# Attention on one Trainium2 core: a bank of values copied whole, its halves joined through a transfer and GpSimd, and the softmax's inverse as a power on GpSimd

## The chip, the core and the metric

The kernel runs on one core of one Trainium2 chip. Its engines are named as in the profile: PE (TensorE, matrix products and transposes through an identity matrix; PEld is its weight load), DVE (VectorE), ACT (ScalarE), POOL (GpSimd) and SP (SyncE, which here only issues transfers). Each engine works through its own list in order; an instruction that waits holds up everything behind it on its engine. SBUF and PSUM are the on-chip memories, both with 128 partitions; PE writes to PSUM. The metric is the device time of one launch in microseconds (us), as the median of several runs.

## What is computed

A two-layer encoder on 1024 tokens of width 1024. Only the attention of the first layer is touched by the change:

```python
q = rmsnorm(q, q_gain); k = rmsnorm(k, k_gain)
q = apply_axial_rope(q, cos, sin) * (HEAD_DIM ** -0.5)
k = apply_axial_rope(k, cos, sin)
...
def attend_block(q_blk):
    scores = jnp.einsum('bkgqd,bksd->bkgqs', q_blk, kt).astype(jnp.float32)
    p = jax.nn.softmax(scores, axis=-1).astype(vt.dtype)
    return jnp.einsum('bkgqs,bksd->bkgqd', p, vt)
...
return o @ w_o
```

There are 16 query heads of width 64 and four key and value heads. After it come a cross-attention and a gated feed-forward part, then a second layer with a pooling mixer; they make up most of the time, and their code is the same before and after.

## The kernel before

All products are done with numbers split in two: `hi` is the value rounded to PE's reduced float32 form, `lo` is the rest, and a product is made of the partial products that matter.

The attention loop works on 128 **units**. A unit is one query head for one block of 128 queries; the units 2n and 2n+1 are the same head for two blocks. Helper `skewed` runs three stages with a lag: in step s it writes down `scores(s)`, then `turn_p(s-2)`, then `values(s-3)`, and the last does something for odd units only, for both blocks of a head at once.

- `scores(u)`: PE makes four products into a PSUM tile `pA` (128 queries by 1024 keys, two such tiles; line 779). DVE takes the row maximum (789), ACT takes the exponential into an SBUF tile `scr` and sums each row at the same time (792), DVE takes the inverse of the sum (794), POOL multiplies the rows by it (795).
- `turn_p(u)`: PE turns the 128 by 1024 probabilities in eight transposes into two banks `pB` (740); ACT writes the `hi` part (673) and DVE the `lo` part (674) of each bank into `PT`.
- `values(u)`, u odd: PE multiplies `PT` with the values of the head in 16 products into one bank `pB` of 128 partitions by 256 queries (1191, 1192). The weights hold the `hi` part of the values in 64 columns and the `lo` part in the other 64, so the head's result is the sum of the upper and lower 64 partitions. ACT copies the lower half to SBUF (1196) and DVE adds the upper half from PSUM to it (1197). The two heads of a pair share one tile `osum`, an even head in partitions 0 to 63 and an odd one in 64 to 127. After an odd head POOL writes the pair's `hi` (1200) and `lo` (1201).

Inside the loop the order on each engine is that of the program as the tile framework lays it out, with its own look ahead; there are no due times here. Transfers are all issued from SP. At the loop's end SP issues the eight loads of the output projection's weights `w_o` (681, each 512 KB through a `scr` tile, then split by ACT and DVE) and the eight loads of the residual `X` (2122). Pool `scr` has six tiles of 128 by 1024. The output projection runs in the order: rows 0 and rows 2 with the first four weight loads, then rows 0 and rows 2 with the last four.

Of the kernel before, what the change touches and what calls it, by code (L numbers as in the profile page):

```python
# [10 lines left out]
F32 = mybir.dt.float32  # L11
F32R = mybir.dt.float32r
AF = mybir.ActivationFunctionType
OP = mybir.AluOpType
AX = mybir.AxisListType

P = 128
# [6 lines left out]
HD = 64  # L24
# [55 lines left out]
def skewed(n, *stages):  # L80

    for step in range(n + max(lag for lag, _ in stages)):
        for lag, stage in stages:
            if 0 <= step - lag < n:
                stage(step - lag)


class Slots:


    def __init__(self, tiles):
        self.tiles = tiles
        self.freed = {(i, h): 0 for i in range(len(tiles)) for h in range(2)}
        self.clock, self.now, self.until = 0, None, None
# [534 lines left out]
class Kernel:  # L629
    def __init__(self, ctx, tc, a, out):  # L630
        self.ctx, self.tc, self.nc, self.a, self.out = ctx, tc, tc.nc, a, out
        pool = lambda name, **k: ctx.enter_context(tc.tile_pool(name=name, bufs=1, **k))
        self.cst = pool("cst")
        self.rp = pool("rslots")
        self.fp = pool("fp")
        self.st = pool("st")
        self.R = Slots([self.rp.tile([P, 2048], F32R, name=f"R{i}") for i in range(N_SLOTS)])
        nc = self.nc
        self.ident = self.cst.tile([P, P], F32, name="ident")
        make_identity(nc, self.ident)  # L640
        self.WT = {}
        self.mh = self.cst.tile([P, 8], F32, name="mh")
        nc.vector.memset(self.mh, -0.5)
        nc.scalar.activation(self.cst.tile([P, 8], F32, name="warm"), self.mh, AF.Square)


# [115 lines left out]
    def attention(self):  # L762
        nc, R, a, tc = self.nc, self.R, self.a, self.tc
# [5 lines left out]
        Q, prs, OT, sums = {}, {}, [], {}  # L769

        def score(u):
            j, hh, i = units[u]
            kv = hh // 4
            c0 = (j % 2 + 2 * i) * P
            q = R.v(Q[kv, j // 2], 4)[:, hh % 4, c0:c0 + P]
            s = self.psA()
            for kh in range(2):
                for part in range(2):
                    nc.tensor.matmul(s[:, kh * 512:(kh + 1) * 512], q,  # L779
                                     R.v(K[part][kh], 4)[:, kv],  # L780
                                     start=part == 0, stop=part == 1)
            return s

        def scores(u):
            if u in prs:
                return
            s = score(u)
            nm = self.stat(1, "nm")
            nc.vector.tensor_reduce(nm, s, axis=AX.X, op=OP.max, negate=True)  # L789
            pr = prs[u] = self.scr()  # L790
            rs = self.stat(1, "sum")
            nc.scalar.activation(pr, s, AF.Exp, bias=nm, accum_out=rs)  # L792
            ri = self.stat(1, "inv")
            nc.vector.reciprocal(ri, rs)  # L794
            nc.gpsimd.tensor_scalar(pr, pr, ri, 1.0, op0=OP.mult, op1=OP.mult)  # L795

        with tc.tile_pool(name="qk", bufs=1, reuse_waits="tile") as qk, self.psum("psq", 1, 6) as self.ps:
# [3 lines left out]
            tabs, at, where = {"Q": tab}, {}, {}  # L801
# [59 lines left out]
            def plan_x(n0, wide, sizes, late=()):  # L861
                c0 = n0 % 512
                for j, w in enumerate(sizes):
                    k0 = sum(sizes[:j])
                    raw, k = ("xraw", n0, k0), ("hT", n0, k0)
                    for t in range(n0 // P, (n0 + wide) // P):
                        at["xkeys"].setdefault(t, []).extend([k] * w)

                    def fetch(raw=raw, k0=k0, w=w):
                        at[raw] = self.scr()[:, :w * wide].rearrange("p (k n) -> p k n", k=w)  # L870
                        nc.sync.dma_start(out=at[raw], in_=xt[k0 * P:(k0 + w) * P, n0:n0 + wide].rearrange("(k p) n -> p k n", p=P))

                    def parts(b):
                        return (R.v(s, 4)[:, b % 4, c0:c0 + wide] for s in hT[n0 // 512][b // 4 * 2:b // 4 * 2 + 2])

                    def high(raw=raw, k0=k0, w=w):
                        for b in range(k0, k0 + w):
                            nc.scalar.activation(list(parts(b))[0], at[raw][:, b - k0], AF.Copy, scale=at["gain"][:, b:b + 1])

                    def low(raw=raw, k0=k0, w=w):  # L880
                        for b in range(k0, k0 + w):
                            hi, lo = parts(b)
                            nc.vector.scalar_tensor_tensor(lo, at[raw][:, b - k0], at["gain"][:, b:b + 1], hi.bitcast(F32),
                                                           op0=OP.mult, op1=OP.subtract)
                        at.pop(raw)
                    plan.add("load", w * wide / 1024, fetch, (), [raw], [("scr", raw)], late=late[j] if late else None)
                    plan.add("copy", w * (wide + 100), high, [raw, "gain"], [k], uses=[raw])
                    plan.add("add", w * (wide + 60), low, [raw, k, "gain"], [k], uses=[raw])
# [280 lines left out]
        self.ps = self.ctx.enter_context(self.psum("ps", 2, 4))  # L1169
        with tc.tile_pool(name="at", bufs=1, reuse_waits="tile") as at:  # L1170
            PT = [[at.tile([P, 2048], F32R, name=f"PT{i}{j}") for j in range(2)] for i in range(2)]
            def parts(u):
                return (x.rearrange("p (a b) -> p a b", a=8) for x in PT[u // 2 % 2])

            def turn_p(u):
                ph, pl = parts(u)
                c = slice(u % 2 * P, (u % 2 + 1) * P)
                self.transposed(prs.pop(u), lambda g, p: self.hi_lo(ph[:, 4 * g:4 * g + 4, c], pl[:, 4 * g:4 * g + 4, c], p))

            def values(u):  # L1180
                j, hh, i = units[u]
                if i == 0:
                    return
                kv = hh // 4
                if hh == 0:
                    OT.append([R.get(), R.get()])
                ph, pl = parts(u)
                o = self.psB()[:, :256]
                for kt in range(NT):
                    v = R.tiles[V[kt // 4]].rearrange("p (k h c) -> p k h c", k=4, h=4)[:, kt % 4, kv, :]  # L1190
                    nc.tensor.matmul(o, v, ph[:, kt], start=kt == 0, stop=False)  # L1191
                    nc.tensor.matmul(o, v, pl[:, kt], start=False, stop=kt == NT - 1)  # L1192
                if hh % 2 == 0:
                    sums[0] = at.tile([P, 256], F32, name="osum", bufs=2)
                oo = sums[0][(hh % 2) * HD:(hh % 2 + 1) * HD]
                nc.scalar.copy(oo, o[HD:])
                nc.vector.tensor_tensor(out=oo, in0=o[:HD], in1=oo, op=OP.add)
                if hh % 2:
                    hi, lo = (R.v(x, 8)[:, hh // 2] for x in OT[j])
                    nc.gpsimd.tensor_scalar(hi, sums[0], 1.0, 1.0, op0=OP.mult, op1=OP.mult)  # L1200
                    nc.gpsimd.tensor_tensor(out=lo, in0=sums[0], in1=hi.bitcast(F32), op=OP.subtract)
                if hh % 4 == 3:
                    if j % 2:
                        R.put(Q[kv, j // 2])

            skewed(len(units), (0, scores), (2, turn_p), (3, values))
            R.put(*V, *K[0], *K[1])
        return OT
# [9 lines left out]
    def cross(self, i, X, steps=None, mixer=None, over={}):  # L1218
# [6 lines left out]
        plan_sums = self.down_sums(i)  # L1225
        q, nf, mem, kT, v, sm, PT, O, wo = {}, D // (2 * P), {}, [], [], {}, {}, {}, {}
        both = lambda t: [(f"X{t}", j) for j in range(2)]
# [158 lines left out]
        def plan_turn(plan, t):  # L1386
# [7 lines left out]
            def part(g, j):  # L1394
                if t % 2 not in PT:
                    PT[t % 2] = [R.get_pair() for _ in range(4)]
                pairs = PT[t % 2][2 * g:2 * g + 2]
                src = sm["ps", t][g].rearrange("p (a b) -> p a b", a=4)
                same = all(one[0] == other[0] for one, other in pairs[:j + 1])
                for ks in [slice(0, 4)] if same else [slice(0, 2), slice(2, 4)]:  # L1400
                    hi, lo = (R.blocks(z, ks, slice(t // 2 * P, (t // 2 + 1) * P)) for z in pairs)
                    self.low(hi, lo, src[:, ks]) if j else self.high(hi, src[:, ks])
            plan.add("turn", 8, emit, both(t), banks, [("B", k) for k in banks])
            for g in range(2):
                k = ("PT", t, g)
                plan.add("copy", 512, partial(part, g, 0), [banks[g]], [k], (), banks[g:g + 1], room=(("PT", t % 2), 8))
# [762 lines left out]
```

## Time and profile before

| what | value |
|---|---|
| median of 3 runs | 2509.84 us (2508.43 to 2512.4) |
| the profiled execution, its own time | 2511.04 us |
| its span in the trace | 2509.3 us |
| PE busy | 2480.5 us, 99% |
| DVE busy | 1982.1 us, 79% |
| ACT busy | 1354.9 us, 54% |
| POOL busy | 387.9 us, 15% |
| the attention loop's row maxima (line 789) | from 177.0 to 525.0 us |

The profile is of one execution. Shares are averages over very different stages: POOL, idle for most of the program, does half of its work in the attention loop. Ends of PE's instructions are modelled, so starts are the better guide to its pace.

### The profile page before, as it was taken

What the parts mean: (1) busy time and instruction counts of PE and PEld (TensorE: products, weight loads), DVE (VectorE), ACT (ScalarE), POOL (GpSimd) and SP (SyncE); (2) the same over time, 40 slices, a digit from 0 to 9 for tenths busy, and PEclk for the clock granted to TensorE, in tenths of its full rate; (3) what the DMA queues carried; (4) which work ended last, traced back from release to release, by engine and by line L of the source; (5) the groups of instructions that cost most, each with busy time, mean ns of one, the idle gap of its engine ahead of it and who ended that gap; (6) DMA issues with size and microseconds to landing.
All of it is one profiled execution on the core that took longest, in us unless ns stands there. A gap on an engine that the chain in (4) does not pass through costs nothing.

```text
span 2509.3 us, 37034 instructions
## 1 busy us (share of the span) xinstructions
PE 2480.5 (99%) x13435; PEld 2126.9 (85%) x13435; DVE 1982.1 (79%) x2963; ACT 1354.9 (54%) x2307; POOL 387.9 (15%) x530
## 2 busy tenths in 40 slices
PE   9999999999999999999999999999999999999998
PEld 8998888888898888888888888889888888887887
DVE  7779999974986379888889776887559988888875
ACT  6558888862555255555555334555435555555542
POOL 5755455431001000000000003102000000000001
PEclk9999999999999999999999999999999999999999
DMA  7100000042595124243358553388223324337852
GB/s 253 43 1 2 1 2 1 1 160 72 181 317 188 54 82 126 84 121 111 85 170 290 196 178 111 124 283 307 73 72 109 114 84 124 108 93 257 275 189 97
DMA packets 309613, 322.29 MB, mean 128 GB/s; under 512 B 13110, under 2 KB 243742, under 8 KB 309430
## 3 DMA queue, kind: packets, MB, share of 16 engines
q1 hardware_dynamic: 309429, 319.92, 39.4%
q8 instruction: 106, 1.74, 0.3%
q14 instruction: 78, 0.63, 0.1%
HBM read 232.48 MB, written 82.58 MB: 126 GB/s over the span
## 4 chain that ended last, share of the span: by engine, by line
PE 85%; DVE 6%; issue 4%; ACT 3%; DMA 2%; POOL 1%; POOLq 0%; SPq 0%; DVEq 0%; ACTq 0%
PE pB L746 21%; PE pB L748 21%; PE pB L747 21%; PE pA L779 4%; PE pB L740 3%; PE pA L748 3%; PE pA L746 3%; PE pA L747 3%; PE pB L1191 2%; PE pB L1192 2%; DVE R L668 1%; DVE nm L789 1%; ACT R L665 1%; PE pB L323 1%; DMA X<-in_ffn_w_up 1%
## 5 line engine op out<-in xcount | busy, mean ns | idle before, releaser
L746 PE MATMUL pB<-R,R 128*128 128x512 f32 (+1 forms) x2764 | 1025.3, 371 | 7.3 <-DVE scr L439 2.3
L748 PE MATMUL pB<-R,R 128*128 128x512 f32 (+1 forms) x2760 | 1017.6, 369 | 1.3 <-DVE R L668 1.2
L747 PE MATMUL pB<-R,R 128*128 128x512 f32 (+1 forms) x2764 | 1018.5, 368 | 0.0
L746 PEld LDWEIGHTS pB<-R,R 128*128 128x128 f32 x2764 | 521.8, 189 | 99.8 <-DVE scr L439 4.0
L748 PEld LDWEIGHTS pB<-R,R 128*128 128x128 f32 x2760 | 521.0, 189 | 88.9 <-DVE R L668 2.6
L747 PEld LDWEIGHTS pB<-R,R 128*128 128x128 f32 x2764 | 522.0, 189 | 85.3 <-DVE R L674 0.3
L665 ACT ACTIVATE R<-scr 128x512 fp32r<-128x512 f32 (+2 forms) x340 | 256.6, 781 | 217.2 <-DMA scr<-Gs 58.8
L668 DVE TENSOR_TENSOR R<-scr,R 128x512 fp32r<-128x512 f32 (+2 forms) x340 | 292.0, 888 | 21.0 <-ACT R L665 20.4
L668 DVE TENSOR_TENSOR R<-X,R 128x512 fp32r<-128x512 f32 x374 | 253.1, 689 | 67.4 <-ACT R L665 66.7
L665 ACT ACTIVATE R<-X 128x512 fp32r<-128x512 f32 x374 | 232.0, 630 | 134.9 <-PE pB L747 65.6
L719 POOL TENSOR_SCALAR ms<-ss 128x1 f32<-128x1 f32 (+1 forms) x53 | 12.9, 244 | 1657.8 <-ACT R L727 1281.3
L437 ACT COPY scr<-pB 128x512 f32<-128x512 f32 x156 | 91.0, 584 | 189.2 <-PE pB L748 183.2
L1760 DVE TENSOR_TENSOR X<-pB,X 128x512 f32<-128x512 f32 (+1 forms) x145 | 99.4, 687 | 85.6 <-PE pB L748 84.8
L795 POOL TENSOR_SCALAR scr<-scr,inv 128x1024 f32<-128x1024 f32 x125 | 140.7, 1126 | 164.0 <-DVE inv L794 158.9
L674 DVE TENSOR_TENSOR PT<-pB,PT 128x512 fp32r<-128x512 f32 x256 | 163.9, 681 | 1.6 <-ACT PT L673 0.6
L792 ACT ACTIVATE scr<-pA,nm 128x1024 f32<-128x1024 f32 x125 | 139.6, 1117 | 41.9 <-DVE nm L789 39.4
L789 DVE TENSOR_REDUCE nm<-pA 128x1 f32<-128x1024 f32 x125 | 152.5, 1220 | 0.4 <-PE pB L740 0.3
L746 PE MATMUL pA<-R,R 128*128 128x512 f32 (+1 forms) x420 | 150.6, 359 | 0.0
L748 PE MATMUL pA<-R,R 128*128 128x512 f32 (+1 forms) x420 | 150.3, 358 | 0.0
L747 PE MATMUL pA<-R,R 128*128 128x512 f32 (+1 forms) x420 | 150.0, 357 | 0.0
L779 PE MATMUL pA<-R,R 128*128 128x512 f32 x512 | 145.1, 405 | 0.0
L673 ACT ACTIVATE PT<-pB 128x512 fp32r<-128x512 f32 x256 | 138.8, 595 | 11.0 <-PE pB L740 8.2
(172 smaller groups left out, 3458.4 us busy)
## 6 DMA issues: line engine op xcount, KB each, us to landing
X<-in_ffn_w_up SPq DMA_DIRECT2D x82, 512.0 KB
Gs<-X SPq DMA_DIRECT2D x105, 256.0 KB
scr<-in_ffn_w_down SPq DMA_DIRECT2D x45, 512.0 KB
scr<-Gs SPq DMA_DIRECT2D x35, 512.0 KB
scr<-in_xattn_w_kv SPq DMA_DIRECT2D x32, 512.0 KB
scr<-Gs SPq DMA_DIRECT2D x42, 384.0 KB
Wt<-scr SPq DMA_DIRECT2D x44, 256.0 KB
Gs<-scr SPq DMA_DIRECT2D x42, 256.0 KB
```

The costliest lines, as they stand in the source:

```text
L665: self.nc.scalar.activation(hi, src, AF.Copy)
L668: self.nc.vector.tensor_tensor(out=lo, in0=src, in1=hi.bitcast(F32), op=OP.subtract)
L673: nc.scalar.activation(hi, src, AF.Copy)
L674: nc.vector.tensor_tensor(out=lo, in0=src, in1=hi.bitcast(F32), op=OP.subtract)
L746: mm(out, ah, bh, start=start, stop=False)
L747: mm(out, ah, bl, start=False, stop=False)
L748: mm(out, al, bh, start=False, stop=stop)
L779: nc.tensor.matmul(s[:, kh * 512:(kh + 1) * 512], q, R.v(K[part][kh], 4)[:, kv], start=part == 0, stop=part == 1)
L789: nc.vector.tensor_reduce(nm, s, axis=AX.X, op=OP.max, negate=True)
L792: nc.scalar.activation(pr, s, AF.Exp, bias=nm, accum_out=rs)
L795: nc.gpsimd.tensor_scalar(pr, pr, ri, 1.0, op0=OP.mult, op1=OP.mult)
L1760: nc.vector.tensor_tensor(out=x, in0=banks[b][:, c], in1=x, op=OP.add)
```

## The change

Three things are edited, all in the attention loop. The inverse of a row sum is now a power with exponent -1 on POOL, with a constant tile `m1`. ACT now copies the whole bank of values, 128 partitions, into a part of one `scr` tile (`halves`) that is held through the loop. A transfer on SP moves the half that lies in the wrong partitions into a tile `crossed`, and POOL adds the two halves; the sum of a pair of heads comes to lie in `total`, from which POOL makes `hi` and `lo` as before.

```diff
+        self.m1 = self.cst.tile([P, 1], F32, name="m1")
+        nc.vector.memset(self.m1, -1.0)
...
-            nc.vector.reciprocal(ri, rs)
+            nc.gpsimd.tensor_tensor(out=ri, in0=rs, in1=self.m1, op=OP.pow)
...
+            halves = self.scr().rearrange("p (a b c) -> p a b c", a=2, b=2)
...
-                if hh % 2 == 0:
-                    sums[0] = at.tile([P, 256], F32, name="osum", bufs=2)
-                oo = sums[0][(hh % 2) * HD:(hh % 2 + 1) * HD]
-                nc.scalar.copy(oo, o[HD:])
-                nc.vector.tensor_tensor(out=oo, in0=o[:HD], in1=oo, op=OP.add)
-                if hh % 2:
+                odd, pair = hh % 2, u // 4 % 2
+                if not odd:
+                    sums["crossed"] = at.tile([P, 256], F32, name="crossed", bufs=2)
+                own, far = halves[:, pair, odd], sums["crossed"]
+                nc.scalar.copy(own, o)
+                mine, other = (slice(HD * odd, HD * odd + HD), slice(HD - HD * odd, P - HD * odd))
+                nc.sync.dma_start(out=far[mine], in_=own[other])
+                total = halves[:, pair, 0]
+                nc.gpsimd.tensor_tensor(out=total[mine], in0=own[mine], in1=far[mine], op=OP.add)
+                if odd:
                     hi, lo = (R.v(x, 8)[:, hh // 2] for x in OT[j])
-                    nc.gpsimd.tensor_scalar(hi, sums[0], 1.0, 1.0, op0=OP.mult, op1=OP.mult)
-                    nc.gpsimd.tensor_tensor(out=lo, in0=sums[0], in1=hi.bitcast(F32), op=OP.subtract)
+                    nc.gpsimd.tensor_scalar(hi, total, 1.0, 1.0, op0=OP.mult, op1=OP.mult)
+                    nc.gpsimd.tensor_tensor(out=lo, in0=total, in1=hi.bitcast(F32), op=OP.subtract)
```

Lines of the changed kernel stand two to seven further down than before. Three places show what moves.

**DVE in the middle of the loop.** `nm` is the row maximum, `inv` the inverse, `osum` the halves' sum, `PT` the `lo` part; the rows cover four units. Before:

```order
L789 TENSOR_REDUCE nm<-pA 128x1
L1197 TENSOR_TENSOR osum<-pB,osum 64x256
L674 TENSOR_TENSOR PT_2587<-pB,PT_2586 128x4x128 x2
L794 RECIPROCAL inv<-sum 128x1
L789 TENSOR_REDUCE nm<-pA 128x1
L674 TENSOR_TENSOR PT_2589<-pB,PT_2588 128x4x128 x2
L794 RECIPROCAL inv<-sum 128x1
L789 TENSOR_REDUCE nm<-pA 128x1
L1197 TENSOR_TENSOR osum<-pB,osum 64x256
L674 TENSOR_TENSOR PT_2589<-pB,PT_2588 128x4x128 x2
L794 RECIPROCAL inv<-sum 128x1
```

and now:

```order
L791 TENSOR_REDUCE nm<-pA 128x1
L676 TENSOR_TENSOR PT_2589<-pB,PT_2588 128x4x128 x2
L791 TENSOR_REDUCE nm<-pA 128x1
L676 TENSOR_TENSOR PT_2589<-pB,PT_2588 128x4x128 x2
L791 TENSOR_REDUCE nm<-pA 128x1
L676 TENSOR_TENSOR PT_2591<-pB,PT_2590 128x4x128 x2
```

The inverses and the additions have left DVE; the row maxima and the `lo` parts keep their order.

**POOL in the middle of the loop**, four units with the end of a pair of heads. Before:

```order
L795 TENSOR_SCALAR scr<-scr,inv 128x1024 x4
L1200 TENSOR_SCALAR R_81<-osum 128x256
L1201 TENSOR_TENSOR R_82<-osum,R_81 128x256
L795 TENSOR_SCALAR scr<-scr,inv 128x1024 x4
L1200 TENSOR_SCALAR R_81<-osum 128x256
```

and now (796 is the power, 797 the multiplication, 1204 the addition of the halves):

```order
L796 TENSOR_TENSOR inv<-sum,m_94 128x1
L797 TENSOR_SCALAR scr<-scr,inv 128x1024
L1204 TENSOR_TENSOR scr<-scr,crossed 64x256
L796 TENSOR_TENSOR inv<-sum,m_94 128x1
L797 TENSOR_SCALAR scr<-scr,inv 128x1024
L796 TENSOR_TENSOR inv<-sum,m_94 128x1
L797 TENSOR_SCALAR scr<-scr,inv 128x1024
L1204 TENSOR_TENSOR scr<-scr,crossed 64x256
L1207 TENSOR_SCALAR R_81<-scr 128x256
L1208 TENSOR_TENSOR R_82<-scr,R_81 128x256
L796 TENSOR_TENSOR inv<-sum,m_94 128x1
L797 TENSOR_SCALAR scr<-scr,inv 128x1024
```

The addition of the halves of an odd unit u stands behind the multiplication of unit u+3 and ahead of the power of unit u+4.

**SP at the loop's end**, with buffer numbers. Before, the weights' loads stand together (the first three and the last are shown), with the residual's behind them:

```order
L681 DMA scr_7320<-in_attn_w_o 128x2x512
L681 DMA scr_7324<-in_attn_w_o 128x2x512
L681 DMA scr_7328<-in_attn_w_o 128x2x512
...
L681 DMA scr_7365<-in_attn_w_o 128x2x512
L2122 DMA X0_7339<-in_x 128x1024
```

and now, from the last crossing but one on:

```order
L1202 DMA crossed_7346<-scr_2592 64x256
L683 DMA scr_7395<-in_attn_w_o 128x2x512
L683 DMA scr_7399<-in_attn_w_o 128x2x512
L1202 DMA crossed_7346<-scr_2592 64x256
L683 DMA scr_7420<-in_attn_w_o 128x2x512
L683 DMA scr_7424<-in_attn_w_o 128x2x512
L2129 DMA X0_7406<-in_x 128x1024
...
L2129 DMA X5_7411<-in_x 128x1024
L683 DMA scr_7428<-in_attn_w_o 128x2x512
L683 DMA scr_7432<-in_attn_w_o 128x2x512
L2129 DMA X6_7412<-in_x 128x1024
```

The loads of the weights now stand behind crossings, and the last two behind six loads of the residual.

## The prediction

> **What bounds the kernel now.** I first asked for the busy time in a window inside the loop (columns: window, length, then PE, PEld, DVE, ACT and POOL busy with counts, PE's clock, DMA share, GB/s), and for the row maxima, of which each unit has one (count, then least/median/most ns, first and last start).
>
> ```profile
> 250.00:300.00 50.00, 50.00 (x359) 44.45 (x358) 47.71 (x82) 42.53 (x81) 24.52 (x26) 1.00 0.01 1
> L789 DVE TENSOR_REDUCE nm<-pA x125: 1204/1225/1227, 177.0 to 525.0; 128x1 f32<-128x1024 f32 x125
> ```
>
> PE and DVE are both near full. 124 steps in 348.0 us make 2.806 us for a unit, 11.23 us for four units, the pattern's period (two heads, one even, one odd), 31 times. Which of the two engines sets it is read from the timeline (start, duration, engine and line, in brackets the idle time before and what ended it).
>
> ```profile
> 354.40 1.12 ACT L792 ACTIVATE scr<-pA,nm 128x1024 f32<-128x1024 f32 x1 [0.57 <-DVE nm L789]
> 354.54 1.10 PE L779 MATMUL pA<-R,R 128*128 128x512 f32 x4
> 355.47 1.04 PE L740 MATMUL pB<-ident,scr 128*128 128x128 f32 x8
> 355.63 0.37 ACT L1196 COPY osum<-pB 64x256 f32<-64x256 f32 x1
> 355.71 0.16 DVE L794 RECIPROCAL inv<-sum 128x1 f32<-128x1 f32 x1 [0.23 <-ACT scr L792]
> 355.81 1.23 DVE L789 TENSOR_REDUCE nm<-pA 128x1 f32<-128x1024 f32 x1
> 356.04 1.12 POOL L795 TENSOR_SCALAR scr<-scr,inv 128x1024 f32<-128x1024 f32 x1 [1.61 <-DVE inv L794]
> 356.27 1.16 PE L779 MATMUL pA<-R,R 128*128 128x512 f32 x4
> 357.07 0.42 DVE L1197 TENSOR_TENSOR osum<-pB,osum 64x256 f32<-64x256 f32 x1
> 357.21 0.86 PEld L740 LDWEIGHTS pB<-ident,scr 128*128 128x128 f32 x8 [0.21 <-POOL scr L795]
> 357.27 1.04 PE L740 MATMUL pB<-ident,scr 128*128 128x128 f32 x8
> 357.52 1.29 DVE L674 TENSOR_TENSOR PT<-pB,PT 128x512 fp32r<-128x512 f32 x2
> 357.57 0.40 POOL L1200 TENSOR_SCALAR R<-osum 128x256 fp32r<-128x256 f32 x1 [0.42 <-DVE osum L1197]
> 358.06 0.73 POOL L1201 TENSOR_TENSOR R<-osum,R 128x256 fp32r<-128x256 f32 x1
> 358.26 0.19 PEld L1191 LDWEIGHTS pB<-PT,R 128*128 128x128 f32 x1 [0.19 <-DVE PT L674]
> 358.72 0.15 DVE L794 RECIPROCAL inv<-sum 128x1 f32<-128x1 f32 x1
> 358.79 1.21 DVE L789 TENSOR_REDUCE nm<-pA 128x1 f32<-128x1024 f32 x1
> 360.12 1.12 ACT L792 ACTIVATE scr<-pA,nm 128x1024 f32<-128x1024 f32 x1 [0.78 <-DVE nm L789]
> 360.25 1.10 PE L779 MATMUL pA<-R,R 128*128 128x512 f32 x4
> 361.18 1.04 PE L740 MATMUL pB<-ident,scr 128*128 128x128 f32 x8
> 361.42 0.16 DVE L794 RECIPROCAL inv<-sum 128x1 f32<-128x1 f32 x1 [0.23 <-ACT scr L792]
> 361.88 1.09 ACT L673 ACTIVATE PT<-pB 128x512 fp32r<-128x512 f32 x2 [0.16 <-PE pB L740]
> ```
>
> DVE sets it, in a ring with ACT. From an inverse at 355.71 to the same place at 361.42: maximum at 355.81, halves added at 357.07, two `lo` parts at 357.52, inverse at 358.72, maximum at 358.79, ACT's exponential at 360.12, the next inverse. DVE's only idle time is the 0.23 in front of an inverse that waits for ACT. PE meanwhile waits 0.21 for POOL and 0.19 for DVE. By starts, scores take 0.93 (354.54 to 355.47), transposes 0.80 (to 356.27) and a values product 1.99 (358.26 to 360.25): 4 x 0.93 + 4 x 0.80 + 2 x 1.99 = 10.9 for four units, and a little less without the wait in it: **PE's own floor is 10.8** against the 11.23 that the loop takes. At most 31 x 0.4 = 13 us can be won here.
>
> **What goes.** Four inverses and two additions leave DVE. It keeps four maxima and four `lo` pairs. A maximum occupies it for at most 1.26 (355.81 to 357.07) and a pair for 1.20 (357.52 to 358.72): 4 x 2.46 = 9.8. DVE no longer binds, PE's 10.8 would, if nothing else came late. Something does.
>
> **What comes.** The power on POOL has a row of its own elsewhere, and so has the width of an addition; the last row shows that 24 partitions cost about what 128 do (1.12 above), so I price the 64-partition addition as line 1201, 0.73, and leave ACT's copy at 0.37.
>
> ```profile
> L721 POOL TENSOR_TENSOR rs<-ms,mh x53: 538/549/887, 552.9 to 2500.4; 128x1 f32<-128x1 f32 x52, 24x1 f32<-24x1 f32 x1
> L673 ACT ACTIVATE PT<-pB 128x512 fp32r<-128x512 f32 x256 | 138.8, 595 | 11.0 <-PE pB L740 8.2
> L2039 POOL TENSOR_SCALAR scr<-scr,rs 24x1024 f32<-24x1024 f32 x1 | 1.1, 1108 | 0.0
> ```
>
> POOL's work for four units: 4 x (0.55 + 0.09 handover + 1.12) + 2 x (0.73 + 0.09) + 0.49 + 0.73 = 9.9. It fits, but the order matters: the addition for u stands ahead of the power of u+4 and waits there for a **transfer**. Behind it are that power, that multiplication, and the transposes of u+4 on PE, on which everything depends. No transfer of 64 KB with a waiter stands in the trace. The nearest are two of 512 KB together between SBUF tiles, on idle queues:
>
> ```profile
> 1540.81 1.55 SPq L2029 DMA_DIRECT2D scr<-X  x2
> 1545.88 1.06 ACT L727 ACTIVATE R<-scr 128x1024 fp32r<-128x1024 f32 x1 [3.09 <-DMA scr<-X]
> 1540.81:1542.20 1.39, 0.57 (x3) 0.36 (x3) 1.06 (x4) 1.39 (x3) 0.81 (x1) 1.00 0.00 0
> 1542.20:1542.60 0.40, 0.40 (x4) 0.40 (x5) 0.40 (x1) 0.40 (x2) 0.00 (x0) 1.00 0.70 195
> 1545.00:1545.30 0.30, 0.30 (x5) 0.30 (x4) 0.23 (x1) 0.00 (x0) 0.00 (x0) 1.00 0.20 82
> 1545.50:1545.70 0.20, 0.20 (x4) 0.20 (x4) 0.20 (x1) 0.00 (x0) 0.00 (x0) 1.00 0.00 0
> ```
>
> For 1.39 us after the issue nothing moves; then 195 GB/s; the last bytes come before 1545.50, and the waiter starts 0.38 later. For 64 KB: 1.39 + 0.33 (at 195 GB/s) + 0.38 + 0.05 from the copy's end to the issue, taken as between 356.04 + 1.12 and PE's start at 357.21, is **2.15 us**. Bounds: 1.7, if data and landing nearly vanish beside the first 1.39; 2.6, with the bytes at the 82 GB/s of the fourth window. I take 2.15, since its first part is a plain row.
>
> [...]
>
> Now the ring that this closes, for an odd unit u with an odd head, starting where POOL has multiplied u: transposes on PE 0.11 (357.16 to 357.27); ACT's first `hi` 0.70 (361.18 to 361.88); DVE's first `lo` 0.63 (0.595 and a handover); the pair 1.20; maximum of u+3 to its exponential 1.33 (358.79 to 360.12); exponential to the copy of u's bank behind it on ACT 1.23 (354.40 to 355.63); the copy 0.37. That is 5.57. Transfer 2.15. Then on POOL the addition 0.82, `hi` 0.49 (357.57 to 358.06), `lo` 0.73, power 0.64, multiplication of u+4 1.12, in all 3.80. **Sum 11.52** for four units. Since each turn needs the one before, this is a period, and it is longer than 11.23, than PE's 10.8 and than POOL's 9.9. The values product of u ends well before its copy is due, and units with even heads lack `hi` and `lo` and so have slack. The loop gives 31 x 0.29 = **+9.0 us**; with 1.7 and 2.6 for the transfer, -5 and +23.
>
> The held `scr` tile costs nothing in the loop: a unit's probabilities live from the exponential to the end of its transposes, at 354.40 to 358.3 for one, under two units' time, and five tiles remain. It and the crossings do touch **the loop's end**, where SP's list is in order:
>
> ```profile
> 516.39 18.63 SPq L681 DMA_DIRECT2D scr<-in_attn_w_o  x8
> 535.08 6.75 SPq L2122 DMA_DIRECT2D X<-in_x  x8
> 540.00:543.00 3.00, 3.00 (x15) 2.50 (x14) 2.03 (x2) 1.06 (x1) 0.54 (x1) 1.00 1.02 404
> 545.55 0.69 DVE L1551 TENSOR_TENSOR X<-pB,X 128x512 f32<-128x512 f32 x1 [1.12 <-DMA X<-in_x]
> 556.55 1.09 PE L323 MATMUL pB<-ident,X 128*128 128x128 f32 x8 [0.56 <-DVE X L318]
> ```
>
> All eight weight loads were issued by 535.0. Now the fifth and sixth wait for the last crossing, about 536.3, and the last two stand behind six loads of the residual: ten times 524 KB at 404 GB/s from about 537.5 on lands near 550.5. The second half of the projection starts near 545.2 and needs the seventh load, split by ACT and DVE, 2.7 us later; the load comes some 3 to 4 us after that, and 0.56 of idle time behind it takes up a part: **+3 us** (0 to 5).
>
> Sum: 9.0 + 3 = +12 on the profiled execution's 2511.04. That one lies 1.2 above the median of the runs, so I forecast a median of 2509.84 + 12 = **2522**.
>
> **Rivals.** *Short transfer* (the other side): at 1.4 us the ring sums to 10.8, PE's floor binds, the loop gives -13 and the end +3, 2500 us. It decides below 1.43 (5.57 + 1.43 + 3.80 = 10.8). For it speaks that 64 KB is an eighth of one of those transfers; against it, the 1.39 before the first byte. 0.08.
> *Even ring*: a transfer of 1.75 to 1.95 makes 11.1 to 11.3, the loop -3 to +3, and with the end 2508 to 2515. 0.20.
> *The ring is not closed*, as ACT or DVE run further ahead than I think, so the change does off the path what it says: then PE's floor too, 2500; against it, both lists are in order and the waits at 354.40 and 360.12 show them without lead. 0.04.
> *Slower POOL*: line 721 reaches 887 ns; with 0.34 more per power and a transfer of 2.6 the ring is 12.3, +33 and more, above 2540. 0.06.
> Forecast 0.62, from 2515 to 2536.
>
> **How the numbers follow.** The range goes from the ring with 1.7 and a cheap end, 2506, to the ring with 2.6 and a full end, 2536; outside are the first and third rivals, the fourth and a little of the forecast, 0.2. Faster by over 0.2% (5 us, about what a measurement of this kernel can tell): 0.12, the rivals on PE's floor. Within: 0.19. Slower: 0.69.
>
> **What would show it.** Row maxima of one unit and the fourth after it 11.5 apart; DVE under 9.8 of them busy; POOL's addition idle ahead of it until a transfer lands, about 2.1 us after the copy, and PE's transposes after an odd pair waiting for POOL by about half a us more than now. At the end PE waiting in the second half of the projection. Wrong would be maxima 10.8 or 12 and more apart, additions that wait for nothing, or the loss outside 177 to 560 us, where no term of mine lies.

## The result, and the profile after

| | before | changed |
|---|---|---|
| median of 6 runs | 2510.2 us (2508.43 to 2512.49) | 2528.0 us (2526.45 to 2530.27) |
| ratio, with its 95% interval | | 1.007 (1.006 to 1.0081) |
| profiled execution: own time, span | 2511.04, 2509.3 us | 2530.27, 2528.5 us |
| first to last row maximum of the loop | 348.0 us | 354.3 us |
| last row maximum to the span's end | 1984.3 us | 1996.4 us |

The change costs 17.8 us, 0.7%. The last two rows say where, for the profiled executions: 6.3 in the loop and 12.1 behind its last maximum; the loop also starts 0.8 later. The stages after the output projection have the same code. PE's first transposes behind that projection start 31.5 after the last maximum before (at 556.55, the row is in the prediction) and 42.2 after it in the changed kernel (574.36): 10.7 of the 12.1 lie ahead of them and are looked for at the loop's end. The other 1.4 lie behind, where the same code took between 1950.8 and 1955.2 us in the fourteen traces of this document, so they can't be put down to the change. The maxima and a window inside the loop, in the views and columns that the prediction used:

```profile
L791 DVE TENSOR_REDUCE nm<-pA x125: 1215/1218/1226, 177.8 to 532.1; 128x1 f32<-128x1024 f32 x125
```

```profile
250.00:300.00 50.00, 48.08 (x344) 42.58 (x343) 40.98 (x52) 39.13 (x76) 39.81 (x52) 1.00 0.05 13
```

DVE fell from 47.71 to 40.98 of 50 us, POOL rose from 24.52 to 39.81, and PE fell from 50.00 to 48.08: DVE was relieved, and PE got less to do per time. A turn is four units, from one row maximum to the fourth after it. The timeline of one turn of the changed kernel, from the copy of an odd head to the next one, cut to the rows of the ring (start, duration, engine, line, in brackets the idle time before):

```profile
360.54 0.37 ACT L1200 COPY scr<-pB 128x256 f32<-128x256 f32 x1
362.95 0.73 POOL L1204 TENSOR_TENSOR scr<-scr,crossed 64x256 f32<-64x256 f32 x1 [0.46 <-ACT PT L675]
363.78 0.41 POOL L1207 TENSOR_SCALAR R<-scr 128x256 fp32r<-128x256 f32 x1
364.27 0.74 POOL L1208 TENSOR_TENSOR R<-scr,R 128x256 fp32r<-128x256 f32 x1
364.97 0.55 POOL L796 TENSOR_TENSOR inv<-sum,m 128x1 f32<-128x1 f32 x1
365.62 1.12 POOL L797 TENSOR_SCALAR scr<-scr,inv 128x1024 f32<-128x1024 f32 x1
366.79 1.09 PE L742 MATMUL pB<-ident,scr 128*128 128x128 f32 x8
367.55 1.09 ACT L675 ACTIVATE PT<-pB 128x512 fp32r<-128x512 f32 x2 [1.15 <-PE pB L742]
368.18 1.29 DVE L676 TENSOR_TENSOR PT<-pB,PT 128x512 fp32r<-128x512 f32 x2 [0.19 <-ACT PT L675]
369.38 1.22 DVE L791 TENSOR_REDUCE nm<-pA 128x1 f32<-128x1024 f32 x1
370.69 1.12 ACT L794 ACTIVATE scr<-pA,nm 128x1024 f32<-128x1024 f32 x1
371.80 0.36 ACT L1200 COPY scr<-pB 128x256 f32<-128x256 f32 x1
```

Each row waits for the one above it; the ring closes in 371.80 - 360.54 = 11.26. The addition starts 2.04 after the copy's end (360.91); in the other ordinary turns it is mostly 2.1. Its bracket names ACT, which had long been done: what it waits for is the transfer. Of the 31 turns, 27 take 11.25 to 11.46 (the median is 11.32), the first 10.71, and three 12.54, 12.94 and 12.54. One of the three, in the timeline, and the DMA queues between 278.6 and 282.0 (packets, MB, share of 16 engines):

```profile
278.30 0.37 ACT L1200 COPY scr<-pB 128x256 f32<-128x256 f32 x1
281.99 0.74 POOL L1204 TENSOR_TENSOR scr<-scr,crossed 64x256 f32<-64x256 f32 x1 [1.74 <-DMA crossed<-scr]
```

```profile
q1 hardware_dynamic: 80, 0.07, 8.2%
q8 instruction: 1, 0.02, 2.4%
```

The addition comes 3.32 after the copy's end (278.67). Beside the 80 packets of the crossing (64 of data, 16 of landing) there is one packet of instructions, and it takes 1.3 us on one of the 16 DMA engines. Such a packet of 16 KB passes about every 18 us, in both kernels. In the three long turns, and in no other, one started 0.8 to 1.1 us behind the copy's end, just ahead of the crossing's first data: the crossing's share on that engine lands late and POOL waits for it.

The loop's end of the changed kernel: SP's list, PE's rows with long waits ahead of them, and windows around them (the last three columns are PE's granted clock, DMA share and GB/s).

```profile
532.37 1.89 SPq L683 DMA_DIRECT2D scr<-in_attn_w_o  x2
536.81 0.47 SPq L1202 DMA_DIRECT2D crossed<-scr  x1
537.40 1.02 SPq L683 DMA_DIRECT2D scr<-in_attn_w_o  x2
545.18 0.47 SPq L1202 DMA_DIRECT2D crossed<-scr  x1
545.76 1.05 SPq L683 DMA_DIRECT2D scr<-in_attn_w_o  x2
546.87 3.33 SPq L2129 DMA_DIRECT2D X<-in_x  x6
550.60 1.71 SPq L683 DMA_DIRECT2D scr<-in_attn_w_o  x2
```

```profile
539.15 1.09 PE L742 MATMUL pB<-ident,scr 128*128 128x128 f32 x8 [2.77 <-POOL scr L797]
563.21 0.80 PE L748 MATMUL pB<-R,R 128*128 128x512 f32 x1 [4.49 <-ACT R L675]
564.47 0.79 PE L749 MATMUL pB<-R,R 128*128 128x512 f32 x1 [0.46 <-DVE R L676]
```

```profile
541.30:544.40 3.10, 3.10 (x14) 3.10 (x15) 2.88 (x3) 1.57 (x2) 0.00 (x0) 0.50 0.21 79
563.20:568.20 5.00, 4.52 (x10) 3.24 (x11) 2.44 (x2) 1.06 (x1) 0.00 (x0) 0.50 0.59 231
```

PE waits twice: 2.77 ahead of the last unit's transposes, for POOL, and 4.95 in the second half of the projection, for the split of the seventh weight load. Behind both waits it was granted half its clock (0.50 in both windows). That is paid too: the last 16 values products start 0.21 apart instead of 0.12 (+1.5), and the next ten projection products 0.43 and more instead of 0.23 (about +2.5).

### The profile page after: what moved, and what is told of

It is laid out like the page before. It is cut to its first block, busy times and chain, and to the rows that moved or that the text cites. A ratio compares the mean times of both kernels' runs of the same rounds, so it can differ in the third digit from the quotient of the medians.

```text
span 2528.5 us, 37163 instructions
## 1 busy us (share of the span) xinstructions
PE 2484.0 (98%) x13435; PEld 2129.2 (84%) x13435; DVE 1947.0 (77%) x2775; ACT 1349.3 (53%) x2307; POOL 502.1 (20%) x719
## 3 DMA queue, kind: packets, MB, share of 16 engines
q8 instruction: 106, 1.74, 0.3%
## 4 chain that ended last, share of the span: by engine, by line
PE 81%; POOL 5%; issue 4%; DVE 4%; ACT 3%; DMA 3%; POOLq 0%; ACTq 0%; SPq 0%; DVEq 0%
PE pB L748 21%; PE pB L750 21%; PE pB L749 21%; PE pA L750 3%; PE pA L748 3%; PE pA L749 3%; PE pB L742 3%; PE pA L781 2%; DVE R L670 2%; POOL scr L797 1%; ACT PT L675 1%; PE pB L1195 1%; PE pB L1194 1%; PE pB L323 1%; ACT R L667 1%
## 5 line engine op out<-in xcount | busy, mean ns | idle before, releaser
L742 PEld LDWEIGHTS pB<-ident,scr 128*128 128x128 f32 x1024 | 116.4, 140 | 40.1 <-POOL scr L797 28.9
L742 PE MATMUL pB<-ident,scr 128*128 128x128 f32 x1024 | 134.6, 274 | 12.7 <-POOL scr L797 9.2
```

Source lines behind the costliest of these rows:

```text
L742: self.nc.tensor.transpose(p[:, k, :], src[:, b * P:(b + 1) * P], self.ident)
```

## The experiments

Each was compared with the kernel before, run beside it on the same chip. "Loop" is from the first to the last row maximum, "rest" from the last one to the span's end, both of the profiled execution. Each of these two is read from a single trace.

| run | median, us | ratio (95%) | loop | rest |
|---|---|---|---|---|
| before | 2510.2 | | 348.0 | 1984.3 |
| changed | 2528.0 | 1.007 (1.006 to 1.0081) | 354.3 | 1996.4 |
| power alone | 2512.14 | 1.0011 (1.0002 to 1.0021) | 349.4 | 1983.4 |
| crossing alone | 2512.1 | 1.001 (1.0001 to 1.0019) | 342.3 | 1990.7 |
| no crossing, one run | 2507.55 | | 339.5 | 1986.3 |
| join behind u+4 | 2551.91 | 1.0172 (1.0157 to 1.0187) | 382.3 | 1992.9 |
| join behind u+5 | 2510.87 | 1.0004 (0.9994 to 1.0013) | 339.7 | 1991.3 |
| weights first | 2524.38 | 1.0051 (1.0038 to 1.0065) | 353.3 | 1985.8 |
| weights first again, one run | 2523.06 | | 354.0 | 1990.3 |
| crossings from ACT | 2525.32 | 1.0056 (1.0042 to 1.0069) | 351.9 | 1990.7 |
| all three | 2507.18 | 0.9985 (0.9977 to 0.9994) | 339.7 | 1986.9 |
| u+5, weights first, inverse on DVE | 2507.16 | 0.9988 (0.9979 to 0.9998) | 339.3 | 1989.5 |
| the same, crossings from ACT | 2504.95 | 0.9978 (0.997 to 0.9987) | 339.3 | 1986.7 |
| before, no inverse, one run | 2503.01 | | 341.6 | 1982.4 |

### The two parts of the change, each alone

The power alone, as an edit to the kernel before (with its constant `m1`):

```diff
-            nc.vector.reciprocal(ri, rs)
+            nc.gpsimd.tensor_tensor(out=ri, in0=rs, in1=self.m1, op=OP.pow)
```

> Only the inverse goes to POOL; the halves are copied and added by ACT and DVE as before, nothing crosses. Theory A (the changed kernel loses by the transfer in the ring and by its crossings in SP's list, and the power itself is a gain since it takes the inverses out of DVE's list): row maxima of a unit and of the fourth after it at most 11.0 apart (before 11.2, changed 11.32 in an ordinary turn), the loop's end as before, median 2498 to 2505. Rival B (the power lengthens the way from the exponential to the transposes by about 0.5 us and this is what costs): spacing 11.2 to 11.5, median 2510 to 2520.

Theory A's part on the power fell, and rival B's ranges were met. Turns take 11.27, the loop 349.4, and the median is 2.7 above that of before. DVE has fewer instructions and no gain comes of it. The timeline shows the way that a unit takes now:

```profile
361.51 1.12 ACT L794 ACTIVATE scr<-pA,nm 128x1024 f32<-128x1024 f32 x1 [0.57 <-DVE nm L791]
362.80 0.55 POOL L796 TENSOR_TENSOR inv<-sum,m 128x1 f32<-128x1 f32 x1 [0.80 <-ACT scr L794]
363.45 1.14 POOL L797 TENSOR_SCALAR scr<-scr,inv 128x1024 f32<-128x1024 f32 x1
364.64 1.09 PE L742 MATMUL pB<-ident,scr 128*128 128x128 f32 x8
```

From the exponential to the transposes 3.13 pass, and PE starts right as POOL ends. Before, the same step took 357.27 - 354.40 = 2.87 by the rows in the prediction, with PE waiting for POOL there too.

Crossing alone: the changed kernel with the line of the inverse put back.

> The changed kernel with the inverse back on DVE; halves cross by the transfer and are added on POOL. Theory A: POOL's part of the ring falls by the power, 0.64, so that the spacing is 10.8 to 11.1 in an ordinary turn, 31 turns give about -8 to -13 against the changed kernel's loop; the loop's end keeps its loss of about 11, since SP's list is the same: median 2512 to 2520. Rival B (the power alone lengthens the loop): spacing 11.2, median 2521. Rival C (the transfer alone sets the ring, whatever POOL does): 11.3, median 2528.

Turns take 10.96 and the loop 342.3, 5.7 less than before, though one turn of 12.18 and two of 11.7 and 11.8 show the packets of instructions again. The rest is 6.4 longer than before, and so the median is as before plus 2.6. Theory A held in the loop; rivals B and C are out. At the end it had the loss at about 11, and it is 6.4: PE waits 1.00 ahead of the last transposes instead of 2.77, with no half clock behind it (1.00 granted from 525 to 543 us), though SP's list has the same order. Each part alone costs 0.1%, both together 0.7%: in the loop the parts alone make +1.4 and -5.7, together +6.3.

Why the power gains nothing was asked with the kernel before, without any inverse:

```diff
-            ri = self.stat(1, "inv")
-            nc.vector.reciprocal(ri, rs)
-            nc.gpsimd.tensor_scalar(pr, pr, ri, 1.0, op0=OP.mult, op1=OP.mult)
+            nc.gpsimd.tensor_scalar(pr, pr, rs, 1.0, op0=OP.mult, op1=OP.mult)
```

> The kernel before without any inverse: POOL multiplies by the sums themselves, so the attention's output is not the reference's; nothing crosses. Theory H (the power alone gained nothing because its 0.55 and a handover lie on the way from the exponential to the transposes, which gave back what DVE's relief had won): with the relief and without the way the spacing falls from 11.20 to 10.96 to 11.0, first to last maximum about 340 to 341. Rival I (DVE's inverses cost nothing before, so that their removal wins nothing): 11.2, first to last maximum 347 to 348.

```profile
L789 DVE TENSOR_REDUCE nm<-pA x125: 1204/1216/1225, 177.2 to 518.8; 128x1 f32<-128x1024 f32 x125
```

Turns of 11.03, loop 341.6: theory H held, though both lie just above its ranges. With the same list on DVE, the power on the way from the exponential to the transposes costs 7.8 us of loop (349.4 - 341.6). The 6.4 that the kernel without an inverse wins over the one before are not DVE's relief alone: its way is shorter, too. From the exponential's start to the multiplication's end it takes 2.43 (360.38 to 362.81), before 2.76 (354.40 to 357.16), with the power 3.08 (361.51 to 364.59). How the 6.4 divide was not separated.

### Is it the transfer, or POOL's work?

The transfer left out:

```diff
-                nc.sync.dma_start(out=far[mine], in_=own[other])
-                nc.gpsimd.tensor_tensor(out=total[mine], in0=own[mine], in1=far[mine], op=OP.add)
+                nc.gpsimd.tensor_tensor(out=total[mine], in0=own[mine], in1=own[mine], op=OP.add)
```

> The changed kernel without the crossing transfers: POOL adds a half to itself, so the attention's output is not the reference's; everything else in the loop is as changed. Theory A (the transfer's 1.97 us in the ring set the pace): spacing falls from 11.32 to PE's floor, 10.8 to 10.9, first to last maximum 354.3 to about 338, and no turn of 12.5 and more, since there is no transfer that instruction fetches could delay. Rival C' (POOL's work in its order, not the transfer, sets the pace): spacing 11.2 to 11.4. At the loop's end no crossing stands in SP's list, but loads 5 to 8 of w_o stand behind six loads of X: the last unit's transposes then wait for nothing over 1 us.

```profile
L791 DVE TENSOR_REDUCE nm<-pA x125: 1214/1217/1226, 179.9 to 519.4; 128x1 f32<-128x1024 f32 x125
```

This kernel leaves out the exchange of the halves, so its output is another. Its 30 full turns take 10.95 to 10.98: PE's floor is **10.96**, not the 10.8 of the prediction; four more kernels below, with other lists on POOL, DVE and ACT, come to 10.95 or 10.96. The transfer sets the pace of the changed kernel; but it has been taken away here, not moved. So the same work with the join (addition, `hi` and `lo`) at another place of POOL's list, while the copy and the transfer stay:

```diff
+            scaled[u] = nc.gpsimd.tensor_scalar(pr, pr, ri, 1.0, op0=OP.mult, op1=OP.mult)
...
+            def join(u):
...
+                with tc.issue_after(scaled[min(u + 4, len(units) - 1)].ins):
+                    nc.gpsimd.tensor_tensor(out=total[mine], in0=own[mine], in1=far[mine], op=OP.add)
...
+            skewed(len(units), (0, scores), (2, turn_p), (3, values), (5, join))
```

> The changed kernel with the same work and the same transfers; only POOL's addition, hi and lo of an odd unit u are queued behind the multiplication of u+4 instead of ahead of the power of u+4. Theory A: the transfer lies beside the power and multiplication of u+4 and leaves the ring; spacing 10.8 to 10.95, also in turns in which an instruction fetch delays the transfer; the loop gives about -15 against the changed kernel, its end keeps the loss: median 2511 to 2516. Rival C' (POOL's sum of work sets the pace): spacing 11.2 to 11.4, median 2525 to 2530.

A clear miss: turns of 12.39 and 2551.91 us, worse than the changed kernel. The transfer is out of the ring, and what came in its place shows in POOL's timeline and in PE's row behind it:

```profile
364.81 1.12 POOL L797 TENSOR_SCALAR scr<-scr,inv 128x1024 f32<-128x1024 f32 x1
366.02 0.74 POOL L1217 TENSOR_TENSOR scr<-scr,crossed 64x256 f32<-64x256 f32 x1
366.85 0.41 POOL L1220 TENSOR_SCALAR R<-scr 128x256 fp32r<-128x256 f32 x1
367.34 0.73 POOL L1221 TENSOR_TENSOR R<-scr,R 128x256 fp32r<-128x256 f32 x1
368.04 0.54 POOL L796 TENSOR_TENSOR inv<-sum,m 128x1 f32<-128x1 f32 x1
369.85 1.09 PE L742 MATMUL pB<-ident,scr 128*128 128x128 f32 x8 [1.19 <-POOL scr L797]
```

Exponentials come in close pairs: 362.88 and 365.06, then 368.35. I had put the join, 2.02 us long, between the two of a close pair. The second one's sums were ready at 366.26, and its power started at 368.04. In the changed kernel the join stands in the long gap, where POOL would idle. So the same edit one unit later, with `u + 5` and lag 6, which is again a long gap:

> As the late join before, but POOL's addition, hi and lo of an odd unit u are queued behind the multiplication of u+5, so in the next gap between two close pairs of exponentials, two units later than in the changed kernel and in the same place of POOL's pattern; work and transfers are the same. Theory A (in the changed kernel the transfer's 1.97 us stands in the ring ahead of the power of u+4): the transfer now has over 5 us more, the spacing falls from 11.32 to PE's 10.96 and no turn is over 11.2; first to last maximum about 339.5 instead of 354.4; at the end the last transposes no longer wait 2.8 for POOL. Median 2508 to 2514. Rival C' (POOL's work, wherever it stands, sets the pace): 11.3 to 12.4, median 2525 or more.

```profile
L791 DVE TENSOR_REDUCE nm<-pA x125: 1211/1216/1226, 179.0 to 518.7; 128x1 f32<-128x1024 f32 x125
```

```profile
PEld pB L742 <- POOL scr L797: 0.4, 2, 0.2
```

30 turns of 10.96 to 10.98, loop 339.7. PE's weight loads for the transposes wait 0.4 us for POOL (the view of waits, from 180 us to the last maximum: total, times, longest); in the changed kernel it is this row:

```profile
PEld pB L742 <- POOL scr L797: 25.3, 55, 2.2
```

Packets of instructions pass as before and delay nothing, since the transfer now has some five us to spare. The work on POOL is the same, so C' is out; the median fell by 17.1 to that of before. The loop is 8.3 shorter than before, and the rest 7.0 longer, which is the other half of the question.

### The loop's end

```diff
-            if t == NT - 2:
+            if t == 0:
                 ws.append(self.load_rows(a["attn_w_o"][0], 1))
```

> The changed kernel, with the last four weight loads of w_o written ahead of all loads of X instead of ahead of the seventh; the loop is the same. Theory D (the seventh load behind six loads of X costs PE its wait of 4.5 and, behind the wait, about 2.6 at a granted clock of 0.5): third addition of the residual 29 to 31 us after the last row maximum instead of 37.0 (before 25.5); median 2519 to 2522. Rival E (the crossings that hold back the loads are the whole loss at the end): 35 to 37, median 2526 to 2529.

> The kernel with the last weight loads ahead of X once more, for a second trace: its profiled execution was 4 us under its three timed ones. Theory J (at the loop's end an instruction fetch either delays the crossing of unit 125 or does not): in an execution of 2523 or more that crossing's addition starts 3 us or more after the copy's end and PE waits over 2 us ahead of the last transposes, with a granted clock near 0.5 behind the wait; in one near 2520 it starts 2.0 after it, as in the first trace. Rival K (the 4 us lie elsewhere, in the loop's turns or after the projection): 2523 or more with that crossing at 2.0.

The wait for the seventh load is gone in both traces: the third addition of the residual comes 26.2 us after the last maximum (before 25.5, changed 37.0). Theory D held for the place. Yet the median fell only by 3.6, to 2524.38, between the ranges of the two theories, and the profiled execution was the lowest of its four, 2520.26. The second trace took 2523.06. PE's row of the first transposes behind the projection and a window behind it, of the first trace:

```profile
567.71 1.09 PE L323 MATMUL pB<-ident,X 128*128 128x128 f32 x8 [3.43 <-DVE X L318]
```

```profile
567.60:571.00 3.40, 3.29 (x19) 2.87 (x20) 1.22 (x3) 2.66 (x6) 0.74 (x2) 1.00 0.20 77
```

and of the second:

```profile
566.28 1.97 PE L323 MATMUL pB<-ident,X 128*128 128x128 f32 x8 [3.69 <-DVE X L318]
```

```profile
568.00:572.00 4.00, 4.00 (x12) 3.18 (x11) 2.48 (x3) 2.01 (x5) 0.74 (x2) 0.53 0.09 36
```

A part of what was won comes back here. The residual's last load now lands 28.6 us after the last maximum (before 23.7, by the packets), the saving of the first sums (`Xq`) stands behind it in SP's list, and the normalisation, which may overwrite a sum only when it is saved, waits for that on DVE: 6.79 ahead of line 318 instead of 3.93. PE waits some 3.5 ahead of these transposes (0.56 before). Behind nearly the same wait the clock stayed at 1.00 once and fell to 0.53 the other time. The crossing of unit 125 was added 2.1 after its copy's end in both traces, so theory J fell and K holds: the second trace's rest is 4.5 longer (1990.3), and all but 0.3 of that lies behind the start of these transposes. The half clock is seen there: it lasted 6.83 us, of which PE was busy 5.49, so by my estimate it makes at most half of that, 2.7; the rest is not settled.

Issuing the crossings from ACT, right behind the copy:

```diff
-                nc.sync.dma_start(out=far[mine], in_=own[other])
+                nc.scalar.dma_start(out=far[mine], in_=own[other])
```

> The changed kernel with the crossings issued from ACT behind the copy instead of from SP; seven weight loads of w_o then stand ahead of X in SP's list and no crossing is among them. Theory D (the end's loss is SP's list): third addition of the residual 25.5 to 30 us after the last maximum instead of 37.0. Rival F (the scr tile that is held costs the end): 34 or more. The loop by theory A: the ring as before with what the issue occupies of ACT, between 0.05 and 0.46 in each turn: spacing 11.3 to 11.8. Median 2517 to 2532.

The third addition came after 32.9, between the two theories, and the loop took 351.9. Weight loads started at 525.04 instead of 532.37, as wanted. But the crossing of unit 125, whose copy ended at 529.18, came late, as it did in the changed kernel. POOL's and PE's rows, and the DMA queues from 529.0 to 533.6:

```profile
533.61 0.72 POOL L1204 TENSOR_TENSOR scr<-scr,crossed 64x256 f32<-64x256 f32 x1 [2.83 <-DMA crossed<-scr]
537.40 1.97 PE L742 MATMUL pB<-ident,scr 128*128 128x128 f32 x8 [3.60 <-POOL scr L797]
```

```profile
q1 hardware_dynamic: 471, 0.91, 61.5%
q10 hardware_dynamic: 80, 0.07, 5.8%
q8 instruction: 1, 0.02, 1.2%
```

The crossing has its own queue now (q10), weight loads run beside it (q1), and a packet of instructions passed at 531.2. Fifteen engines had brought their share of the crossing by 531.1, the one with the packet at 532.6. The fifteen came 1.96 behind the copy's end where 1.62 is usual in this trace, so the loads made some 0.3 of the delay there; the engine with the packet came 3.41 behind it. POOL started 1.02 after that instead of some 0.45, which stays unexplained. So the end hangs on whether such a packet meets the last crossings (the addition came 3.6 and 4.4 behind the copy's end with one, 2.1 without), as long as the transfer stands in the ring. With the join at u+5 this goes away. All three edits together:

> The changed kernel with all three edits: join behind the multiplication of u+5, crossings issued from ACT, last weight loads ahead of X. Theories A and D together: spacing 10.96 to 11.05, first to last maximum 339.5 to 342, third addition of the residual 25 to 28 after the last maximum: median 2500 to 2505, faster than both kernels. If either theory is wrong the median stays at 2510 or above.

Loop 339.7 and the third addition after 25.5, as expected; the median, 2507.18, is 2 above the range, since the rest is still 2.6 longer than before. With the inverse back on DVE, crossings from SP and then from ACT:

> Crossing with the inverse back on DVE, join behind the multiplication of u+5, last weight loads ahead of X, crossings still issued from SP. Theories A and D: spacing 10.96, no turn over 11.2, loop 339.5 to 340.5; at the end neither a wait for the seventh load nor a late last power; from the last maximum to the span's end at most 2 over that of before (1984.3): median 2502 to 2507. If the crossings in SP's list cost by themselves, the end keeps 5 or more and the median is 2507 to 2511.

> The same with the crossings issued from ACT: the best version so far (2507.2) with the inverse on DVE instead of the power on POOL. Theory A (with the transfer out of the ring PE's floor binds, and the power on POOL is worth nothing): spacing 10.96, median 2503 to 2508, no different from the version with the power. Rival G (the inverses bind DVE again: 4 x 2.46 + 4 x 0.15 + waits for ACT): spacing 11.1 to 11.3, median 2511 or more.

```profile
L791 DVE TENSOR_REDUCE nm<-pA x125: 1214/1222/1227, 177.5 to 516.8; 128x1 f32<-128x1024 f32 x125
```

```profile
549.00:553.00 4.00, 3.67 (x14) 3.17 (x15) 1.82 (x3) 3.09 (x6) 0.75 (x2) 0.62 0.17 66
```

Both loops take 339.3, so theory A held and G is out: PE's floor binds with the inverse on either engine, and the power brings nothing in the loop. From SP the rest is 5.2 longer than before and the median 2507.16, which is the second of the two cases expected: the crossings in SP's list cost something by themselves. From ACT the median is **2504.95**, 5.2 us under the kernel before, run beside it (2510.13). It is 2.2 below the version with the power, where theory A had no difference, but the intervals of the two ratios overlap and the loops differ by only 0.4. So the whole bank copied, crossed and added on POOL beats both kernels once the join has a gap of its own and the loads their order. What is left of the loss at the end (2.4) contains the clock of 0.62 behind a wait of 1.97 ahead of the first transposes; the residual's last load lands 26.1 after the last maximum, still 2.4 later than before.

## Why the prediction was right, and which step was mis-sized

- **The ring** was right, and every term can be read in the turn shown above. Predicted 11.52, measured 11.26 there, 11.32 in the median. Transfer with its handover 2.04 for 2.15; exponential to copy 1.11 for 1.23; POOL's four steps to the multiplication (0.83, 0.49, 0.70, 0.65) together 2.67 for 2.68. Removing the transfer, giving it a gap, or taking the power out of the ring brings 10.96, so that this ring and nothing else set the pace.
- **The loop's +9.0** came as +6.3: 31 x 0.12 = 3.7 from the ordinary turns, and 2.9 more from disturbed ones (three turns in the changed kernel exceed the median by 4.1 in all, a few before by 1.2); a shorter first turn takes some of it back. The first was sized too high, the second I hadn't foreseen.
- **PE's floor** of 10.8 was 10.96. A transfer short enough would have given a loop 8.5 us shorter than before, as without the crossing, and not 13: that rival was priced too well. No run shows the transfer of 1.4 us that it took; in the changed kernel the shortest, with its handover, was 2.04.
- **DVE** was to be under 9.8 of a turn: over the whole loop it is busy 297.27 of 354.30 us, 9.6 of a turn. (The 40.98 of 50 above would make 9.3, but that window holds a long turn.)
- **The loop's end** is the term that was mis-sized: +3 with 5 as its upper bound, measured 12.1 in the profiled execution, 10.7 of them ahead of the transposes behind the projection. The place was right, PE did wait in the second half of the projection for the seventh load, and for 4.95 where "3 to 4" less 0.56 was said. Two things were left out. The last unit has the same ring as all others, and I let the loop end as it did before: its power stood behind the addition of unit 125, which came 3.6 after the copy's end (531.76 to 535.32, with a packet of instructions at 532.6; 2.1 in the two traces of weights first, which have the same weight loads beside it and no packet), and PE waited 2.77. And each wait was priced as its length, while PE ran behind it at half clock: about 4 us in all.
- **The sum** of +12 against 17.8 measured is right in sign and in its range, with the loop 2.7 too dear and the end 9 too cheap. That it lies within the range is partly luck: the range went up to 2536 for a transfer of 2.6, which it was not, and this room took up the end's loss, which is 7 above its own bound.

What stays open: the 2.4 to 2.6 that the end keeps even in the best versions. The scr tile that is held through the loop leaves five for the weight loads; a version without it wasn't tried. Which executions meet the half clock can't be told from the runs without a trace, since in the traces a wait of 1.97 had it behind it and one of 3.43 had not (last section).

## What to carry to other kernels

In the turn from 278.30 POOL's addition waited 1.74 us for its transfer, and the power that stands behind it in POOL's list, whose sums were ready at 281.71, started at 284.01: what counts is what is queued behind such a wait. The same addition cost 15 us of loop ahead of the next power, nothing one gap later, and 43 us against that in the wrong half of the pattern (382.3 against 339.7): look for the gap in which the engine would idle anyway. Price two edits together as a ring, not one by one. At the end of a loop follow the list of the transfer queue and give PE's waits there their length and the slow stretch behind them.

## What the runs showed of the hardware

- A 64 KB transfer between SBUF tiles: in ordinary turns of the changed kernel the waiter starts 2.1 (2.04 and more) after the copy that feeds it has ended; by the packets its first byte moves 1.15 to 1.19 and its last has come 1.60 to 1.65 after that end.
- Instructions were loaded in packets, before and in the changed kernel: in the loop one of 16 KB about every 18 us, 0.9 to 1.5 us each on one DMA engine, and between them ones of 8 KB, 0.3 to 0.6 us each. Each of the three of 16 KB that started just ahead of a crossing's data in the changed kernel's loop (0.8 to 1.1 behind the copy's end) delayed the waiter by 1.2 to 1.6; with the join behind u+5, which leaves the transfer some five us of slack, no full turn was over 10.98.
- PE's granted clock behind waits: 0.50 behind 2.77, 0.62 (mean of 4 us) behind 1.97, 0.53 (mean of 4 us) behind 3.69, and still 1.00 behind 3.43. The traces' records of the clock show that length alone didn't decide. In the changed kernel the half clock came in stretches of 3.41 us or two of them (541.07 to 544.48 and 561.55 to 568.37), and in its trace and that of before the changes lie whole multiples of 3.41 apart (six from 541.07 to 561.55). What went with it here is how much PE was busy (second number) in the window of 3.41 before. Here is one window of the changed kernel, one of the last version, and two of weights first, whose wait of 3.43 falls into both (counted on from this trace's change of clock at 60.7):

```profile
537.65:541.07 3.42, 1.48 (x9) 1.04 (x9) 0.54 (x1) 1.17 (x3) 2.07 (x3) 1.00 0.81 237
546.57:549.99 3.42, 1.45 (x10) 0.99 (x9) 1.89 (x2) 0.08 (x1) 0.00 (x0) 1.00 0.04 16
562.46:565.87 3.41, 1.83 (x9) 1.17 (x7) 0.00 (x0) 0.00 (x0) 0.00 (x0) 1.00 0.62 238
565.87:569.28 3.41, 1.57 (x11) 1.48 (x12) 1.89 (x2) 0.94 (x1) 0.00 (x0) 1.00 0.05 20
```

  Behind the first two the clock was halved, behind the other two it stayed full. From 300 to 620 us the traces of before and of the changed kernel, cut into such windows from a change of clock on, have two at full clock with at most 1.48 us of work, both in the changed kernel: the first one above and the one from 558.13 to 561.55, with 0.60. Behind these two the clock was halved, behind no other at full clock; the next least had 1.65 (319.20 to 322.61 in the changed kernel). So a wait of 1.97 was followed by half the clock and one of 3.43 was not, with 1.45 us of work in the window against 1.83 and 1.57. This is a reading of this stage: in a later one of the changed kernel half clock (0.50 from 1595.79 to 1599.20) also follows a window that is shown as busy throughout (3.42 of 3.42 us).
